# A hybrid decoder layer on one core: which engine evicts the transposes of the second norm, a PSUM bank per tile at the start, and a new order of all instructions

## The chip, the core and the metric

The kernel runs on one core of a Trainium2 chip. The metric is the time of one execution on the device in microseconds (us). The core's engines run side by side and meet at semaphores: TensorE (PE; PEld is its weight load), VectorE (DVE), ScalarE (ACT), GpSimd (POOL) and SyncE (SP), which issues the DMAs. The kernel before has a median of 1169.25 us in 3 runs (1168.5 to 1170.7).

## The reference

One decoder layer on a sequence of 1024 rows of width 1024, in float32. Cut to what matters here:

```python
h = modulate(rms_norm(x), shift1, scale1)            # first norm
q, k, v, z, lx, ly, a, b = split(h @ w_in)           # 4 heads of 128; lx, ly: 512 wide
o = gated_delta_rule_chunked(l2(q), l2(k), v, decay(a), beta(b))   # chunks, state S per head
gdn = rms_norm(o) * silu(z)
xr = conv(lx); r = sigmoid(gate_a(xr)); i = sigmoid(gate_x(xr))
log_a = 8 * r * log_sigmoid(lam)
lru = scan(exp(log_a), sqrt(-expm1(2 * log_a)) * (i * xr)) * gelu(ly)
lru = rms_norm(lru)                                  # over the 512 channels of the group
x = x + gate1 * (concat(lru, gdn) @ w_out)
h2 = modulate(rms_norm(x), shift2, scale2)           # second norm
x = x + gate2 * (relu(h2 @ w_up) ** 2 @ w_down)
out = rms_norm(x)
```

## The kernel before

**Stages.** The kernel works on whole matrices, 128 rows or columns at a time. It normalises x and transposes it on PE (tiles `xTq`, `xTp`) into two rounded halves `hh` and `hl`; projects it, head by head, with three matmuls a product (high by high, low by high, high by low): `k_p`, `z_p`, `q_p`, `v_p`, `lx_p`, `ly_p`; inverts the triangular chunk matrices (`it`, `iy`, `iw`, `iz`: tiny matmuls, with DVE between them); runs the chain of states of each head (`ch`, `cho`, the state `S`, the values `nv`); and for each of four channel tiles the recurrence `lru` (L1377 to L1427): 24 `gate` matmuls, 8 evictions by tanh into `ta` and `ti`, then exp, tanh, square and square root on ACT, products and a scan on DVE, the square of the result (`lsq`) on ACT, and the sum of squares `msum` on POOL. `lrus` (L1452 to L1456) are 8 tiny matmuls over `msum`; they give the factor `rsl` of the norm of the recurrence. The out-projection has a part for the delta rule (`wg`, 16 groups of 12 matmuls) that doesn't need `lrus`, and a part for the recurrence (`wl`, 16 groups of 12), which is multiplied by `rsl` as it is added to x. With two `wl` groups of a row tile t done, `norm2(t)` (L1519 to L1547) squares and scales that tile, transposes it in 8 PE transposes into two PSUM banks of four tiles each (`h2T{t}_0`, `h2T{t}_1`), and evicts each 128x128 tile with scale and shift into `h2r`, the odd ones on ACT and the even ones on DVE. The MLP then runs as seven products of sums of blocks (`upx`, `upy`, `upz`, then `dn`), from 545 us to the end.

**Order.** Nothing is issued as the code stands. Each call appends an `Op` to a `Recorder`, and `schedule` (L293 to L451) lays out all engines with a model: durations, latencies between engines, PE's clock, free buffers. Among the ready operations of an engine it takes the one with the smallest priority, and the priority of each operation that is not part of the backbone on PE is moved by its own entry of `_SHIFTS`, a table of 8374 numbers. `emit` (L453 to L461) issues the operations in the order found, so in the trace nearly every instruction has line L461, groups recorded with `mms` L639; tiles tell them apart. On the chip each engine runs its own queue in that order and stops at the first instruction whose inputs or whose PSUM bank are not free. PSUM has 8 buffers of one bank (`ps`). The names in the rows below end in a running number where a tile is one of several.

**The first transposes.** `xquarter(q, k0)` (L908 to L918) transposes two 128-column tiles of two row tiles of x, four PE transposes into one bank, and evicts each half of the bank twice, once on ACT (`hh`) and once on DVE (`hl`).

Of the kernel before, what the change touches and what calls it, by code (L numbers as in the profile page):

```python
# [13 lines left out]
F32 = mybir.dt.float32  # L14
# [40 lines left out]
OVER = {"DVE": 0.08, "ACT": 0.10, "POOL": 0.03}  # L55
RESERVE = {"b": 11, "ps": 2, "u": 1, "c": 2}
# [67 lines left out]
def dram_box(ap):  # L124
# [7 lines left out]
    'c-p;Nd7MsV|Gw^X&hyL|W8XszB~kViWvT328?qFo^(EON@<v4VvQ(5T*%gHdMTjhg$X@n@A-fqf^UQN!zw4R*&+~qcKYq8*d}cZ4d+z)GF4y<E?&tWOD'  # L132
    ';c&|xskh0cQ>Q>wX@V5F@sDNp1^4&;Sf4GubYUw$h%}(J4>?YOmyZu<3jlpPMN1e=iCq7h&Ra@=488h-GbhBTy?V2@4h)Z`)|A2hFB}BPUhEX;jEdFA0'
    'u6(N3+v1a%Jwxsu3L={WaPMX-G1j+rTZ)9axSIZYow>>z1+6J`ib}&giSGV^?zft<H$B0}}At%?;d~-5Q_rT|9|>1pZ2|#-7+>VKZ$DY)ktRFts8NM8{'
    ';O+JRBBdq&NSDP|NZp%mJnD*9n2s$_TPt&AENY-UCd!8OCuR%d=<y4mR%%vO=Iyu}IFp79<>@tnPmGq=8tZsm<=G8{7ozocEqi?{=;cos*sf^<%1vy2L'
    'CVm7fFy0|~3_r`|o+-3vYM3-YKnqxcPkNjzxWADwq@@E}0+0<u+Xi?4aSw=B5<<FROv!w0H_SyHbZpK@9K3Yk>XvOr%5#+|J_y)h=B_7A~*ocAH%+8V0'
    'n8oGjnN})V2@UPU%n!{)7Bc(cv1Ug7jFP5{bC%a^Uh}LsA~F)UP%fHgYnli%Z5Jd(yJxMA9Lp-feCDO-W6@~lsOS-HW<^s2jWl0rJj7%a(!E!B3Dc3rY'
    'PLHonJRdlSE57lElQdnkii>ll6k|t87-4NG;)rcu-P5pEHIl{8`U|LEo>jBzjN3f>GU)MQPSyU#yFoi$4y(@M26Sexzp`qu41{<8!gS<c9h-1)zJ;vCG'
    'oM%jotjfzRyW!1lqF#AHif>n=i8*dZ3-#*ZUOR>>^xaJ<P?srZz5chXs0NuZXr_0~=PfZrZWY*;vbUT%XaETkPN5s3&h?1zd=1VIA(X9yVoFLvem&r)O'
    '42JAQ75MK9Z4Xd3N=%N)-H`y4xFpHO7ia*3T|3dzs)Sc^rtJyKrYDTswAghO^Q7x3@MLH02ZpbVRtd}eC&yU02FG4tD<oM8KKr@d_RVv_C56WMQZCg0F'  # L140
    'ngN<(jTXYF(fM$U$Hb(LPJT~DX*Ykhf^`$MLsN}|MzF>Fb3pz}2=sX^(if7$%ENT8k6}-Ssct;tO%2UqU(UP_#mu45wt`iAm4T<!Qdf9U#qoQ4G3Nv^-'
    'd$b*s^&2bMFEc0DTHKQL9?E5Z9UT^7cKb+k9<&Yc5%x!m^9;wZG@j;GW$q$7SuyKC%OQL_YiHJZ+rsY1{DLXUo4=I}X_=qcAGFrOc))f*PvjM1l{H_Ym'
    '6wdR*l7&%p(J{`H{5+fiy^!d%lHqs@OLhV9<lpux|fCxZrhNHiwGqQ!HMuo<`ll8W6m<DS0BPyMi@rAYPK0l;9>JU@@VHhIGh7m+^H`#D95jv4}S?S9`'
    ')9n(;S7OwmgzUeQ>8&NC>yZcE<p-2*;R>874nkgc3uJml`_FL8b+kdW}PK(E<f91q}m7y&m?n0B&+3lMulmA@VvQ%vH8yA^b=Rr9Q`Sd8?Xf$@Qp=FVs'
    'Wo2=PWR#myB?H*~t7xIA6Jj9|N4(}V@JQO|uFseBfzh5Q9gaeVEL;2lDfs1PFP*n%;<AdmFJY93}Sl-KMJaXS{9Zrbg`cm=g}S0XGE<)cQXhPTRD$ZT%'
    'okkBq<C7e&_7VBk-TOamg2R0UFj7_MD1L4A<AsC0!UWIT~)WBXY=Pnj8%k4vUlo0u}jo9<H0cYEue8x86i*~2oZl`isbO&Fy{dq=zPtC53#eCZ~*9vxV'
    'j;YJxrU<7P53SIKYb}}IjO8x-w;g6zvkqS6^LB~7AM<&V2h}T!upLVCSzfeO$ambnYdv!;>e`p=Vz}DDD}0N4`Gz7}A8QfP7u|??*jXVqaT(Rziq0}-a'
    'UEXA4)c$xo-oo4qY7_oCmqn8h3uN>8;qJte4DR0tJp|!PI6D$vZjH$ORW2JQhlA`Pth_q4=yp}=EGn+ONhG5Tg%>dHXkzwIDw83`;>4vKRV(w9!5XzW2'
    ')2Iovw<hsJu%=rn=W%;t%!lo%vSSuu*yPwlX`c{$JSXp&T8CX-;|Py7Rhs+I!7&%^`Ea>@xFBQFW0gO<r%O`5C1`Rl*HIS5+&Qm=ewkwJ|$Gzj+(nRtb'
    '~zgq=<|)nH3!0hS^QZ=hW0Rj(dSxyyOfIp7ZB6V7vZOmVmiLs{My35@A^ksjFQW?(c(#xwHPa0W-`q?|ktHl_xiXA6%C1^?z_f#+Junt^Se4Q%ld2Z`-'  # L150
# [1759 lines left out]
```

## Time and profile before

| | |
|---|---|
| median of 3 runs | 1169.25 us |
| the profiled execution's own time | 1167.61 us |
| its span | 1165.8 us |
| mean granted PE clock | 0.99 |
| ACT table loads | 8 |
| matmuls of the MLP | 545 us to 1159 us |

The span is the time from the first to the last instruction of the profile; the rest of the execution, 1.8 us, lies around it. A row of a timeline has start and length in us, engine, line, operation, output and inputs, shapes and count; in brackets stands the idle time of the engine ahead of it and what ended that. A row that stands for several instructions has their total. Matmuls overlap, so the pitch between two starts, not the length, is what a matmul costs.

### The profile page before, as it was taken

The page shows a single profiled execution, that of the slowest core. Times are in us where ns is not written, and L with a number is a line of the kernel's source. Part 1 is how long each engine was busy: PE and PEld are TensorE (multiplying, and loading weights), DVE is VectorE, ACT ScalarE, POOL GpSimd, SP SyncE. Part 2 cuts the span into 40 slices and gives each one's busy share as a digit, 9 for nine tenths or more (in the row PEclk, how much of TensorE's full clock was granted, in tenths as well). Part 3 has the DMA queues.
Part 4 walks back from the last instruction along what each step waited for, and adds up shares of the span by engine and source line. Part 5 has one row for each costly group of instructions (what it writes and reads, how often), then busy time and mean ns, then how long its engine had stood idle before and what let it go on. Part 6 is the DMA issues. An engine that isn't in the chain of part 4 may idle for free.

```text
span 1165.8 us, 16532 instructions
## 1 busy us (share of the span) xinstructions
PE 1139.4 (98%) x6288; PEld 974.9 (84%) x6288; DVE 839.0 (72%) x1143; ACT 613.5 (53%) x961; POOL 275.1 (24%) x161
## 2 busy tenths in 40 slices
PE   8999998999999998999999999999999999999997
PEld 5889997999999987777888888888788888888886
DVE  4749897778878888668776787666794376974663
ACT  5627624354667795367646455445754333352542
POOL 1100101110112325000011142223322057931330
PEclk9999998999999998999999999999999999999999
DMA  9506824355462254032268787768999766865532
GB/s 344 201 12 203 328 86 151 91 166 174 159 199 91 109 219 160 37 134 84 77 208 283 243 304 239 243 208 271 374 405 388 270 233 236 287 228 176 179 137 82
DMA packets 126256, 233.75 MB, mean 200 GB/s; under 512 B 10785, under 2 KB 49886, under 8 KB 126178
## 3 DMA queue, kind: packets, MB, share of 16 engines
q1 hardware_dynamic: 126178, 232.71, 57.5%
q8 instruction: 49, 0.80, 0.3%
q14 instruction: 29, 0.24, 0.1%
HBM read 173.93 MB, written 58.74 MB: 200 GB/s over the span
## 4 chain that ended last, share of the span: by engine, by line
PE 78%; DVE 11%; ACT 6%; issue 2%; POOL 1%; DMA 1%; SPq 0%; POOLq 0%; ACTq 0%; DVEq 0%
PE dn L461 26%; PE upx L461 14%; PE upz L461 7%; PE k_p L461 4%; PE upy L461 4%; PE q_p L461 3%; PE v_p L461 3%; PE wl L461 3%; PE lx_p L461 2%; PE ch L461 2%; PE ly_p L461 2%; PE cho L461 1%; PE wg L461 1%; ACT ta L461 1%; DVE xr L461 1%
## 5 line engine op out<-in xcount | busy, mean ns | idle before, releaser
L461 PE MATMUL upx<-h2h,U 128*128 128x512 f32 x512 | 167.8, 394 | 0.0
L461 PEld LDWEIGHTS upx<-h2h,U 128*128 128x128 f32 x512 | 96.3, 188 | 22.4
L461 POOL TENSOR_TENSOR wd<-wd,wd 128x512 f32<-128x512 f32 x32 | 51.7, 1618 | 255.0 <-DMA wd<-in_w_down_dram 217.9
L461 PE MATMUL upx<-h2l,U 128*128 128x512 f32 x256 | 100.8, 394 | 0.0
L461 DVE TENSOR_TENSOR U<-wu,U 128x512 fp32r<-128x512 f32 x112 | 84.5, 771 | 22.1 <-ACT U L461 21.5
L461 ACT ACTIVATE act<-act 128x512 f32<-128x512 f32 x112 | 69.8, 631 | 44.7 <-DVE act L461 40.8
L461 PE MATMUL upz<-h2h,U 128*128 128x512 f32 x256 | 85.0, 394 | 0.0
L461 ACT CAST U<-wu 128x512 fp32r<-128x512 f32 x112 | 66.5, 616 | 24.7 <-DVE wu L461 16.8
L461 PEld LDWEIGHTS upx<-h2l,U 128*128 128x128 f32 x256 | 48.1, 188 | 11.4 <-issue 0.2
L461 PEld LDWEIGHTS upz<-h2h,U 128*128 128x128 f32 x256 | 48.1, 188 | 11.1
L461 PE MATMUL upz<-h2l,U 128*128 128x512 f32 x128 | 50.4, 393 | 0.0
L461 DVE TENSOR_TENSOR act<-upz,ek 128x512 f32<-128x512 f32 x32 | 22.0, 687 | 37.6 <-PE upz L461 34.2
L461 PE MATMUL upy<-h2h,U 128*128 128x512 f32 x128 | 43.0, 397 | 0.6 <-DVE U L461 0.6
L461 ACT COPY ek<-upx 128x512 f32<-128x512 f32 x48 | 27.7, 583 | 29.0 <-PE upx L461 29.0
L461 DVE TENSOR_TENSOR wu<-wu,wu 128x512 f32<-128x512 f32 x48 | 36.9, 774 | 1.4 <-DMA wu<-in_w_up_dram 1.2
L461 ACT ACTIVATE vn<-ch,bcoef 128x128 f32<-128x128 f32 x32 | 11.6, 365 | 42.0 <-PE ch L461 41.8
L461 PE MATMUL q_p<-hl,q_wh 128*128 128x342 f32 x96 | 33.2, 345 | 0.0
L461 POOL TENSOR_TENSOR fin<-xb,fnw 128x512 f32<-128x512 f32 x11 | 22.2, 2023 | 45.1 <-DVE xb L461 26.9
L461 PE MATMUL q_p<-hh,q_wl 128*128 128x342 f32 x96 | 32.6, 339 | 0.0
L461 PE MATMUL q_p<-hh,q_wh 128*128 128x342 f32 x96 | 32.5, 339 | 0.0
L461 PE MATMUL v_p<-hh,v_wh 128*128 128x342 f32 x96 | 31.9, 333 | 0.0
L461 POOL TENSOR_TENSOR R<-R,R_5o 128x1024 f32<-128x1024 f32 x8 | 23.1, 2887 | 37.1 <-DMA R_5o<-in_w_down_dram 37.1
(587 smaller groups left out, 3622.3 us busy)
## 6 DMA issues: line engine op xcount, KB each, us to landing
L<-aod SPq DMA_DIRECT2D x56, 512.0 KB, 4.3
R<-in_w_down_dram SPq DMA_DIRECT2D x40, 512.0 KB, 7.0
wu<-in_w_up_dram SPq DMA_DIRECT2D x32, 512.0 KB, 5.2
aod<-as SPq DMA_DIRECT2D x64, 256.0 KB, 3.2
wd<-in_w_down_dram SPq DMA_DIRECT2D x32, 512.0 KB, 6.1
aod<-act SPq DMA_DIRECT2D x48, 256.0 KB, 2.1
x<-in_x_dram SPq DMA_DIRECT2D x16, 512.0 KB, 6.0
sc_w<-in_w_mod_dram SPq DMA_DIRECT2D x16, 512.0 KB, 4.3
```

The source lines that it names most:

```text
L461: op.fn(*[res(v) for v in op.a], **{n: res(v) for n, v in op.k.items()})
```

## The change

Four edits.

1. In `norm2` all four tiles of a bank are evicted by one engine: ACT where t + g is odd, DVE where it is even. The number of evictions on each engine stays 32.
2. In `xquarter` each of the two 128-column tiles has a bank of its own, of which half is used.
3. The model in `schedule` charges 1.28 us for a change of function table on ACT (`Op.func`), lets DVE and ACT start later, and puts off an operation on a PSUM bank until the last accesses of the other engines to that bank have ended.
4. `_SHIFTS` is another table, so the order of all engines is another.

```diff
+TABLE = 1.28
...
 _SHIFTS = (
-    'c-p;Nd7MsV|Gw^X&hyL|W8XszB~kViWvT328?qFo^(EON@<v4VvQ(5T*%gHdMTjhg$X@n@A-fqf^UQN!zw4R*&+~qcKYq8*d}cZ4d+z)GF4y<E?&tWOD'
+    'c-p;NXLuFWy8hOhGzcXW30?5es~}a1VCWn`L7Ef+QBXiQqI8rhND~wk2pttfX;OtylwL!ZlF%U}p``8X?Cd@Bo_FWo`{zE-?0Y9a&g99HWY2uF*80l(z'
...
+        op.func = (2 if AF.Sqrt in a else 1 if AF.Exp in a or AF.Tanh in a else 0) if eng == "ACT" else 0
...
+        now["ACT"], now["DVE"] = T_INIT + TABLE, T_INIT + 1.1
+        table, actend = 1, 0.0
+        banks = {}
...
+            bank = [b for b in op.bufs if b.tag == "ps"]
+            at = max((f + lat(ops[j], op) for b in bank for g, (f, j) in banks.get(b, {}).items() if g != e), default=0.0)
+            if at > t + 1e-6:
+                heapq.heappush(fut[e], (at, i))
+                continue
...
+                if op.func and op.func != table:
+                    t, table = max(t, actend + TABLE), op.func
...
+                actend = fin if e == "ACT" else actend
+                for b in bank:
+                    banks.setdefault(b, {})[e] = (fin, i)
...
     def xquarter(q, k0):
-        px = ps(f"xTq{k0}_{q}")
         for i in range(2):
+            px = ps(f"xTq{k0}_{q}{i}")
             for j in range(2):
-                tr(px[:, (2 * i + j) * P:(2 * i + j + 1) * P], xt[2 * q + j][:, (k0 + i) * P:(k0 + i + 1) * P], ident)
+                tr(px[:, j * P:(j + 1) * P], xt[2 * q + j][:, (k0 + i) * P:(k0 + i + 1) * P], ident)
...
-            A.activation(a[:, s], px[:, d], AF.Identity, scale=sc)
+            A.activation(a[:, s], px[:, 0:256], AF.Identity, scale=sc)
...
-                    if j:
+                    if (t + g) % 2:
                         A.activation(rv[:, j, :], pk, AF.Identity, scale=sc, bias=sh)
                     else:
                         V.tensor_scalar(rv[:, j, :], pk, sc, sh, op0=ALU.mult, op1=ALU.add)
```

The instructions are the same in kind and almost in number (5754 matmul rows and 8 table loads on both sides); their order differs on every engine up to the second norm. From the first matmul of the up-projection on, PE's order is the same but for one row. Three places follow, the second of them on two engines.

**Second norm, PE, row tile 1.** Before, PE's queue had the eight transposes of the tile together, among the matmuls `wl21` and `wl30`:

```order
L461 MATMUL wl21_4996<-wo3l_4859,lch01_4694 128x512
L461 MATMUL h2T1_0_5014<-ident_72,h2_1_4985 128x128 x3
L461 MATMUL h2T1_1_5019<-ident_72,h2_1_4985 128x128 x3
L461 MATMUL h2T1_0_5014<-ident_72,h2_1_4985 128x128
L461 MATMUL h2T1_1_5019<-ident_72,h2_1_4985 128x128
L461 MATMUL wl21_4996<-wo3h_4842,lcl01_4845 128x512
```

After, at the same place in PE's queue:

```order
L475 MATMUL wl21_4990<-wo2l_4652,lch01_4691 128x512
L475 MATMUL h2T1_0_5003<-ident_72,h2_1_4966 128x128
L475 MATMUL h2T1_1_5005<-ident_72,h2_1_4966 128x128
L475 MATMUL h2T1_0_5003<-ident_72,h2_1_4966 128x128
L475 MATMUL h2T1_1_5005<-ident_72,h2_1_4966 128x128 x3
L475 MATMUL wl21_4990<-wo2h_4642,lcl01_4697 128x512
L475 MATMUL wl21_4990<-wo3h_4777,lch01_4691 128x512
L475 MATMUL wl21_4990<-wo3l_4848,lch01_4691 128x512
L475 MATMUL wl21_4990<-wo3h_4777,lcl01_4697 128x512
L475 MATMUL h2T1_0_5003<-ident_72,h2_1_4966 128x128 x2
L475 MATMUL wl30_5023<-wo0h_4802,lch00_4552 128x512
```

The last two transposes into bank 0 have moved behind four matmuls of 512 columns; the others stay together.

**Last recurrence, ACT, evictions of the last gates.** Before, ACT's queue from the first of the eight evictions of the last channel tile (`ti3`, `ta3` from `gate300` to `gate35121`) on:

```order
L461 ACTIVATE ti3_4539<-gate301_4513,hxb_693 64x512
L461 ACTIVATE ti3_4539<-gate35121_4528,hxb_693 64x512
L461 ACTIVATE ti3_4539<-gate300_4511,hxb_693 64x512
L461 ACTIVATE ta3_4556<-gate301_4513,hab_691 64x512
L461 ACTIVATE ti3_4539<-gate35120_4526,hxb_693 64x512
L461 ACT_TABLE_LOAD
L461 ACTIVATE ta2_4390<-ta2_4390,c2_769 128x1024
L461 ACT_TABLE_LOAD
L461 ACTIVATE tg3_4506<-tg3_4506 128x1024
L461 ACTIVATE ta3_4556<-gate35121_4528,hab_691 64x512
```

After, ACT's queue ahead of and at the first of them:

```order
L475 CAST xrh3_4545<-xr3_4489 128x1024
L475 CAST lch00_4552<-lcm1_4482 128x512
L475 CAST lch10_4556<-lcm1_4482 128x512
L475 ACT_TABLE_LOAD
L475 ACTIVATE tg3_4511<-tg3_4511 128x1024
L475 ACTIVATE ti3_4583<-gate300_4574,hxb_682 64x512
L475 ACTIVATE ti3_4583<-gate301_4576,hxb_682 64x512
L475 ACTIVATE ta3_4602<-gate300_4574,hab_675 64x512
L475 ACTIVATE ta3_4602<-gate301_4576,hab_675 64x512
L475 ACTIVATE lsq2_4616<-ly2_st_4192 128x1024
```

Both table loads, the square root of the third recurrence (`ta2`) and the tanh of `tg3` now stand ahead of all eight evictions; the square `lsq2` of the third recurrence has come between them.

**Last recurrence, PE, `lrus`.** Before, `lrus` stood ahead of the last 48 of the 192 `wg` matmuls:

```order
L461 MATMUL wg51_4752<-wo7h_4353,gch11_4471 128x512
L461 MATMUL wg51_4752<-wo7l_4372,gch11_4471 128x512
L461 MATMUL wg51_4752<-wo7h_4353,gcl11_4519 128x512
L461 MATMUL lrus_4770<-ones_110,msum_3905 128x1 x8
L461 MATMUL wg60_4786<-wo4h_4133,gch10_4187 128x512
L461 MATMUL wg60_4786<-wo4l_4235,gch10_4187 128x512
```

After, in PE's queue:

```order
L475 MATMUL wg61_4788<-wo4l_4330,gch10_4506 128x512
L475 MATMUL wg61_4788<-wo4h_4239,gcl10_4517 128x512
L475 MATMUL wg61_4788<-wo5h_4393,gch10_4506 128x512
L475 MATMUL lrus_4793<-ones_114,msum_3906 128x1 x8
L475 MATMUL wg61_4788<-wo5l_4404,gch10_4506 128x512
L475 MATMUL wg61_4788<-wo5h_4393,gcl10_4517 128x512
```

It has moved 16 `wg` matmuls down. The last gate matmul has moved too: between it and `lrus` there stand 102 `wg` matmuls now, 136 before.

**First chain, PE.** The first matmul of the chains (`ch0_0`, from the values `nv0` of head 0) stood among the tiny matmuls of the inverse (`iw1`, `iw2`) before:

```order
L639 MATMUL iw1_2173<-aw0_1924,LT_1279 64x64 x3
L639 MATMUL iw2_2146<-aw1_1915,LT_1279 64x64
L461 MATMUL ch0_0_2267<-nv0_2254,LT_1279 128x128
L639 MATMUL iw2_2146<-aw1_1915,LT_1279 64x64 x3
L461 MATMUL q1_p2_2010<-hh6_428,q1_wl_1737 128x342
```

After, in PE's queue:

```order
L475 MATMUL v1_p2_2354<-hh5_497,v1_wh_1742 128x342
L475 MATMUL v1_p2_2354<-hl5_505,v1_wh_1742 128x342
L475 MATMUL ch0_0_2383<-nv0_2351,LT_1324 128x128
L475 MATMUL v1_p2_2354<-hh5_497,v1_wl_2255 128x342
L475 MATMUL v1_p2_2354<-hh6_531,v1_wh_1742 128x342
```

It has moved behind the inverse's last matmuls and a good part of the projection `v1_p2`.

More of the change, by code (lines that the diff above doesn't have):

```diff
@@ L136 @@
[L136 to L150, printed above, removed]
@@ L196 @@
[L196 to L198 removed]
+    'c-p;NXLuFWy8hOhGzcXW30?5es~}a1VCWn`L7Ef+QBXiQqI8rhND~wk2pttfX;OtylwL!ZlF%U}p``8X?Cd@Bo_FWo`{zE-?0Y9a&g99HWY2uF*80l(z'
+    '3-YyCKjQ)H9^YC<D}|VGGY*hW-70qr9Q?AX(@e>h5af*8-~|Y5>aZ0yoxJ0i^cduPN6rpSjBNAd5(1Om6!GE4E{o$gxKWg(p;|MU+VDvb&nP&hCi8+I4'
@@ new lines @@
+    'dC`VMEfv<dnpSq$<ycJe&0Fz_ZiO!jmgKpOD(*MWQDnWld_(^PL!tbZa-#5*OgrjMlPIl&na7fFjZi^HPgIq_~=c9x7P&$j%otpYN9TvI&y$)$>v>3d#'
+    'JGo*8A8q;1Xm*8Lgh-YP8}ZJ&l3h0Q*4@Yy)5loQ_bXfJ1y`r;EzHFl`8>U_$NdTja}1j!z(OFxRu8I!DrX@BzXhVrT9OMOL-b3`kBq0!y<Fyk+ELYiZ'
+    '4dMXxLv&Bk}aCMTl8RKzW*6WTijYxc_%gaFhvV`c-@~%E_EXG5te8~5rCBMYT6x7r{Y>}gBgRLw?>p4;+E7&zjX2=JU*E3(@T=%jfbb_qYC4!IZSlvdh'
+    '>*=oh+N<sw_q12W>G-TmYKqZJCAoh!$E)S~JAFPYQbypR>XLa(^_K~{WM*}>N%qTM))tIa^JQ&zL1VV(Mp`Picvj0i>1oB|v@ubwbAPLPsiaKHx`SO<f'
+    '~l$r(yWTI$2=k(u@&#*4Yfg@$p{&Oe|kn(ORN;sw6^=2WDSr3^0sQC;*EUfY}}IZ@~u9rPDy9!oHbR>Tj#8GnJ&b5cDdiMhGUF(G}@!OF9^H6OY~(aVH'
@@ new lines @@
+    'TB|yzc^u&AQ-u-71HNo<5nCWEryYz{*HXw>D#MW(mo{H@M`Q>;8w^>wZ78k^7*T<=Sk$>rJsztj=-=argi~BHoo`)pk{P|B!jl)j8u$w0FOf9iQFSo#N'
+    '{0nw3$*HxP|7j$3D}1J*-tQ1<Z5f$sCJWA5J=|J(9X=16Y?v%jxy<_bJE_gS?vg0RXe>e}I1ZbryVRPwC#b;9?IO+NK&)}+iw@M0Kdm{&2&{23LkerA~'
+    '3z_o2c9+XG_tc%{7mO_53s%xh8n)^NTmgjF@InP9IPtPUa6f@c<4v#P3)Z(J!F=8E$(ae<p@G-=k%6R=>R~ZuIb6YXKj#3XROw+rGsNupYl*SHxY!;Js'
+    '%$IVq9{bG8Xz#5k$FqY`-Z~4*J=whC9_vfa{L<aabJcuib;BBtR>x;B-$zIV&tB9=g6CHD)a*}vkyb0SKk`~9d>-F+^Fwp5S;3o$3BIn<TDti9Nk!Q!h'
+    'kQ}8Nv39>_KwTCf&JNyef1FR>F-_Zo0)YweYCrSd#k&QtB$L6dfklf=`)dld?;+D`6^2ntDr=Bx?>VDnQINaKYPMa$!zK?ZFaRjl=*nqcf<VMS`5vcoG'
@@ new lines @@
+    '5LinVd7Xn)S@r%=?Zb{|(|X6!&n;w*jl<CSJg0mXbPFvQ-)FkZKLZal}~@Es=-F%UUceXAolr5h<pj2?qE+!{1oVue);2id2TYC10~DM_3oo6#Kb?z39'
+    '(*j<5z`Ju$Gg<2(Z`dP^z_%VCaPTxv)e*&rq^V>9+)CARaoCAf<G@&XY=>q-)-6LFd-@~L#x*Ht&2f^)b)q<KwJtcohX8j9)C%!tx0f{tKIP?_MH##E!'
+    'RJmNhHvs*cxpBB?BgW6ECMB4H1lknkJ`BI`d*9;8c+=t3Xk|0%;KRHY2^Lm&Lmt^AB7L}@Is~}xpO34Wr%EV1;vw9|dq?_)m8mJ|BfQ9O?{Hb>;7kZ(B'
+    ')RT*hb_sbRk1<6JQ%`j<Jx*;=f66G;S-$dj7I`E)6r`NQt2?M6qok9RmJcPbZlvz0@oEe^<tepC-J+j9(@W)`)|}^JW36m4MoV>Lw!W;B*l$DCdexY0V'
+    '6|GH_Nz9sOA0Yl=HNB?fqt&VDr?Glwv}gaqbnm)i;MeMmr-T)MD>eYL9h|b>)M7?mpLjuXr$4`NKuFMSfi=D926CDP-co{G*C|^Lw4#x#zpBC{EM0?(R'
@@ new lines @@
+    '!tERi4W+sbG8}Kk7>Ck}LFVwNR((TPjSKlZL^IBsOTU5h;DygHz$pi*WfyF00#8ovVC?ZTL~9NfIVXwA|!pZ%Q25LSH#76J(_>B|D4~avjr*`sxie&)6'
+    'bfBP=LH#mG@9p`z3>M2c6>!&hpW+)&HaTzNyF2FVR1qphrAt++8n*X6p0%XV3<pX!Y|EGR)&Qe}-As=EG3n(8m4r!18}SP9kSEblW?&d~SEINJ^?PU`d'
+    'LVzMpg_@^9Oggdr4fv24JY_cY&$7ANF)1#_m3kwa&FE*lsW6L1r+<)a9TXc|Ygc1MhIksHMY;k(zacr>^Q`l47%)T;2t_TU@x7*M5C7rQP=g&o~Y(<p4'
+    'B2!gIc9xMcpP!VGNGamjfqPkfA3L7oImZ@_WCyO{37LIw)Req(3nj$^iyb0S!iZI^abJ8qUqK3!U*5wja*-bBgM#uAqS@18_}44+e^d^FJ3Er_7VVrKB'
+    '^+CHlWW*1UD#9h61!_-ri?^!nZ-{^N&y+piVc(P`YzTHmx3i95q7<*s(gr+cd0oRT3(!l+bS#f(NsQ_R#+nk(Nrx*sPs`w*}LM%k<K#%Dv~X|qG}swuv'
@@ new lines @@
+    'PM-H7hO=<<u=>z4eY<)T{L_j8nDsr|Os$rK-tyYLFU6wiC)O@&tl6;lV}bmm+%3RcR`kv+AqQsdK6hXA#UkQQ7gzhcUj+Yxh;h7T~O>;UiT@%1d?i4l^'
+    'bXz50#3Pgb-_g|jP$>9V?uYN2;Zf378u^x%riNH%?NLA6vPrL;QC?w`r;&Ft8#c+WBX{)4kmQXyjKJW^LLkT<m(?bQ(~>U1QtpRSPY2+kEFUMA%nJI1*'
+    'umrz@0kwr%^GYV0Ueap_@N$Mho>{i$zLwJo3mE<|nWSq*6W@ID5Y7eflzfT|wNr8`9V4{&8sw%3dIHjtqY~o2D=_^xtkJb1IC1kGj#Zrk-KkHGf$inOm'
+    'n=x7L%6(?|Na@Z|%CP6BNs4&nE<I;RGj)LaycXxR6w`4)1~Ti561kq@ytGtr6Y=|~0?gk~*0v@J7>-vyiLA#t#wO;Xw`ZU?=eL+XbP=b5Ip1{F-7;4CI'
+    'Chk8RjB+*h7zgTk>wpGY9FG_ZWL47<&IQVjhLmG95n$MaGnndIO^Eyg=32l#-=jY^&>fYOGYJJQmB}_a@CXNEOwHw50`%O2{~sv&lyrd|3+^VW$mw)DX'
@@ new lines @@
+    'Jf1-$;#67s>ej861wz)EVOyh~`UKwKvp9M6jx|gZgehb7v2`Kz=!bU!<1|<{h+pVbx_G?34z~qZ;IMSr|+FO5u1DaS2rzwPyGVpU{tI@eseMin3V^l*e'
+    'i^F|?w3owMvOUXFdAI?bfgQ1XDYtjnKG__H{_Z_3Nk$S7tE)w9$I6i`ad<4i+y>ciQQSKN%K)8kFY7PZI_*D)St$aD;8C5_oD!nu|@suSyOI;N^c>PuB'
+    'vpH`PuW!Bj~=}M~s*lF}qpX(d!JojZhJ8cFt)}Md%ICCH5KXf=B>3gDf5c9n?^S2-IzJhEaKPezzs2)^K_1Q(Msn@6zqNpJHs-u`qbQ+>cQ)Ry{v8p(c'
+    '=Sy0zlXzSsw+WF;a)zq3lXPd_jgVDpu(}}Gw8+BOQiSNSTy9Z)G$Hm?X6~%yXUSF#=Kc$2;83!Z^Qfn4Qq6wM%(;%L^x_d_{6c{IcAU(@EUJ(1nB!q;7'
+    'Iohs6)YbhckH1$Yp?QuASVByhf9caCEzAob87Q27n$~qHvjtX-v<#$f{5^%nN)+!uL2Ru&xb4Xr<Mab80BM3n(*3zGKjW$h)5>#IvzEc)#V(SlO0<`vK'
@@ L199 @@
+    'O#iqFC42<SEs2;XnVI)|;dRy>OE}Jq>=v){^Wo4zu{zd@AS>oS$Fs)Mn0wN!y&A^s)Gw+`{SMLItk31eMrY$MbB32h>gpn1S~k+xnl&`QOk#0O#*NnRt'
+    'tOuQB~#I<^gGO&IbNs}SngSK~3B3_Y4UE86k68_7SWGiDWKlH+kpaiw#~T4FKCd=*8>x;tUM)t-E02DMy_tY_RCF%O<FhRvisabz#^CYdNY53`Ab9?T('
+    'k>ny+G7svB%%FgcBd*R}BZ2KzJ!T)56Q(F&qs~ya)L29UDe|;!%(goEdPDQHk<!#kTddo1?P1Tp;x+RrktO{pk)g(ek${an|F+gOZuiByNtJOKX5YFp6'
+    'TQyguBp$KWJaH2togST}rVP<1Q4?d-K($Gf+Tr*fh16+PQ#<E96D5<l+=%G*5VzD!T~_@YT0j&&'
 )
@@ L225 @@
     __slots__ = ("adj", "work", "port", "eng", "fn", "a", "k", "outs", "ins", "dur", "bb", "preds", "succs", "allocs", "bufs", "lst", "ready",
-                 "need", "load", "bias", "pri", "tiny", "tail")
+                 "need", "load", "bias", "pri", "tiny", "tail", "func")
 class Recorder:
@@ L908, in xquarter @@
     def xquarter(q, k0):
-        px = ps(f"xTq{k0}_{q}")
         for i in range(2):
+            px = ps(f"xTq{k0}_{q}{i}")
             for j in range(2):
-                tr(px[:, (2 * i + j) * P:(2 * i + j + 1) * P], xt[2 * q + j][:, (k0 + i) * P:(k0 + i + 1) * P], ident)
-        for i in range(2):
+                tr(px[:, j * P:(j + 1) * P], xt[2 * q + j][:, (k0 + i) * P:(k0 + i + 1) * P], ident)
             a, b = hT[k0 + i]
-            s, d, sc = slice(q * 256, q * 256 + 256), slice(i * 256, i * 256 + 256), A1[:, k0 + i:k0 + i + 1]
-            A.activation(a[:, s], px[:, d], AF.Identity, scale=sc)
-            V.scalar_tensor_tensor(out=b[:, s], in0=px[:, d], scalar=sc, in1=a[:, s].bitcast(F32),
+            s, sc = slice(q * 256, q * 256 + 256), A1[:, k0 + i:k0 + i + 1]
+            A.activation(a[:, s], px[:, 0:256], AF.Identity, scale=sc)
+            V.scalar_tensor_tensor(out=b[:, s], in0=px[:, 0:256], scalar=sc, in1=a[:, s].bitcast(F32),
                                    op0=ALU.mult, op1=ALU.subtract)
```

81 lines of the change are left out of this document (30 added, 51 removed).

## The prediction

> **What bounds the kernel now.** The first view is the page's table of busy time, since it says whether any engine is full; the second is the list of what PE waited for, since that engine is the full one.
>
> ```profile
> PE 1139.4 (98%) x6288; PEld 974.9 (84%) x6288; DVE 839.0 (72%) x1143; ACT 613.5 (53%) x961; POOL 275.1 (24%) x161
> ```
>
> ```profile
> PE lrus L461 <- POOL msum L461: 3.8, 1, 3.8
> PE ch L461 <- DVE nv L461: 3.0, 1, 3.0
> PE h2T L461 <- ACT h2r L461: 2.9, 7, 0.7
> PE warm L461 <- DVE ones L461: 2.3, 1, 2.3
> PE h2T L461 <- DVE h2r L461: 1.7, 3, 0.7
> PE cho L461 <- issue: 1.3, 1, 1.3
> PE it L639 <- DVE xnc L461: 0.9, 1, 0.9
> PE sc_r L461 <- DMA sc_w<-in_w_mod_dram: 0.8, 1, 0.8
> ```
>
> The columns of the second are total, times and longest, in us. PE is the bound, and the change neither adds nor removes a matmul, so all that it can win is time in which PE stands still or runs slowly, and all that it can lose is new time of that kind. The eight rows add up to 16.7 us: 3.8 at `lrus`, 4.6 at `h2T`, 3.9 around the inverse and the first chain, 4.4 elsewhere. Busy time hides a second loss, which the windows show. Their columns are the stretch, its length, busy time of PE, PEld, DVE, ACT and POOL, then the granted clock of PE, the DMA share and GB/s.
>
> ```profile
> 179.45:182.86 3.41, 3.41 (x13) 2.63 (x13) 3.28 (x5) 2.95 (x5) 0.00 (x0) 0.50 0.80 267
> 196.52:206.76 10.24, 10.24 (x55) 9.39 (x55) 3.29 (x6) 2.14 (x4) 0.00 (x0) 0.50 0.17 54
> ...
> 459.34:466.17 6.83, 6.83 (x21) 5.58 (x21) 1.99 (x3) 4.37 (x7) 6.83 (x4) 0.50 0.74 269
> ...
> 545.00:850.00 305.00, 304.19 (x1312) 245.86 (x1311) 221.60 (x297) 175.84 (x295) 66.67 (x40) 1.00 0.71 242
> ```
>
> In the first three stretches PE is fully busy at half clock, so half of each is lost: 1.7, 5.1 and 3.4 us. The second begins after the wait for `nv`, the third right after the wait for `msum`; a wait there is paid twice. The last row is the first half of the MLP: 304.19 of 305 us busy at full clock. There is nothing to win there, PE's order in it stays, and the term for it is zero. The whole prize is in the first 545 us, and at most some 27 us.
>
> **The change part by part.** *Evictions of the second norm.* The rows of one row tile, PE and ACT:
>
> ```profile
> 485.53 0.39 PE L461 MATMUL wl<-wo0h,lch 128*128 128x512 f32 x1
> ...
> 485.76 0.39 PE L461 MATMUL wl<-wo0l,lch 128*128 128x512 f32 x1
> ...
> 486.23 0.82 PE L461 MATMUL h2T<-ident,h 128*128 128x128 f32 x6
> 486.65 0.89 ACT L461 ACTIVATE h2r<-h2T,sh,sc 128x128 f32<-128x128 f32 x2
> ...
> 487.61 0.44 PE L461 MATMUL h2T<-ident,h 128*128 128x128 f32 x2 [0.56 <-DVE h2r L461]
> ```
>
> Six transposes go out; then evictions begin on the banks, and the two transposes left stand until ACT and DVE have let go of their bank. Ten such waits make the 4.6 us. With one engine to a bank an eviction no longer waits for the other engine's, and in the new order the transposes that are late stand behind four `wl` matmuls, at a pitch of 0.23 us (485.53 to 485.76) some 0.9 us of work, against two ACT evictions of 0.89 us in the row of 486.65. The cover is thus just long enough; where it isn't, the wait is a few tenths, and it may still come ten times. A bank is now drained in series: four ACT evictions by that row are 1.8 us where two engines took half of it. The cost is hidden by the `wl` groups, each of 12 matmuls or 2.8 us; the eight PSUM buffers decide if it isn't. Bounds: no gain, since such waits could only be renamed, and −6.2 us, the ten waits and 0.16 us of restart at each. I take **−4**.
>
> *The wait for `lrus`.* The last gate matmuls on PE, then ACT, DVE and POOL:
>
> ```profile
> 421.97 0.40 PE L639 MATMUL gate<-xrh,gw 64*128 64x512 f32 x2
> ```
>
> ```profile
> 427.54 1.28 ACT L461 ACT_TABLE_LOAD   x1
> 428.83 1.06 ACT L461 ACTIVATE ta<-ta 128x1024 f32<-128x1024 f32 x1
> ...
> 432.29 1.96 ACT L461 ACTIVATE ta<-gate,hab 64x512 f32<-64x512 f32 x3
> 434.29 1.25 ACT L461 ACTIVATE aa<-ta,nc 128x1024 f32<-128x1024 f32 x1
> 435.57 1.25 ACT L461 ACTIVATE ta<-ta,c 128x1024 f32<-128x1024 f32 x1
> 436.72 1.04 ACT L461 ACTIVATE a<-aa 128x1024 f32<-128x1024 f32 x1
> ...
> 442.40 1.05 ACT L461 CAST wo2h<-wo 128x1024 fp32r<-128x1024 f32 x1 [3.69 <-DVE wo L461]
> ...
> 446.25 2.17 ACT L461 CAST lch<-lcm 128x512 fp32r<-128x512 f32 x4
> ...
> 454.52 1.06 ACT L461 ACTIVATE lsq<-ly_st 128x1024 f32<-128x1024 f32 x1 [2.93 <-DVE ly_st L461]
> ```
>
> ```profile
> 437.79 1.23 DVE L461 SCALAR_TENSOR_TENSOR ta<-a,ta 128x1024 f32<-128x1024 f32 x1 [1.59 <-ACT a L461]
> 438.93 3.44 DVE L461 SCALAR_TENSOR_TENSOR wo<-wo,cols,g_bc 128x1024 f32<-128x1024 f32 x1
> 442.29 0.68 DVE L461 TENSOR_TENSOR x<-wg,x 128x512 f32<-128x512 f32 x1
> 442.89 0.68 DVE L461 TENSOR_SCALAR ta<-ta 128x1024 f32<-128x1024 f32 x1
> ...
> 447.60 1.72 DVE L461 TENSOR_TENSOR xr<-xr,ta 128x1024 f32<-128x1024 f32 x1
> ...
> 450.43 2.28 DVE L461 TENSOR_TENSOR_SCAN xr<-aa,xr 128x1024 f32<-128x1024 f32 x1
> ...
> 453.21 1.21 DVE L461 TENSOR_TENSOR ly_st<-ly_st,xr 128x1024 f32<-128x1024 f32 x1
> ```
>
> ```profile
> 455.72 2.35 POOL L461 TENSOR_TENSOR msum<-msum,lsq 128x1024 f32<-128x1024 f32 x1 [7.49 <-ACT lsq L461]
> ```
>
> ```profile
> 458.12 2.49 PE L461 MATMUL lrus<-ones,msum 128*128 128x1 f32 x16 [3.77 <-POOL msum L461]
> ```
>
> From the end of the last gates (422.3) to `lrus` (458.1) the chain takes 35.8 us, and 136 `wg` matmuls at 0.23 us cover only 32 of them. In the new order 102 stand there, 23.7 us, so the chain must lose 12 us to keep PE busy. Added up along the new order: four evictions at 0.65, 2.6; `wo2h` 1.05; `aa`, `a`, tanh 3.5; the product `ta` 1.23; an addition to x and the maximum 1.4; the root 1.06, its table load lying beside DVE's work behind two `lch` casts (1.1 + 1.28 against 1.23 + 1.4); four additions to x begun under the root, 2.7 less 1.06, 1.7; the product with xr 1.72; a cast's remainder 0.68; scan 2.28; an addition 0.68; `ly_st` 1.21; `lsq` 1.06; `msum` 2.35. That is **22.5**. What is gone is what stood in the chain before: two loads with a root and a tanh between the gate evictions (4.7 us), and three scalings `wo` between `ta` and the scan, one of them 3.44 us, which now stand ahead of or behind it. The margin is 1.2 us; hand-offs between engines, seven of them, eat most of it. If it holds, the 3.77 us go and the 3.4 us of half clock with them. DVE's additions to x wait for `wg` groups, but such a group is done before PE gets to `lrus`. I take **−6.5**; bounds −7.2 and, by the old length of the chain, 35.8 − 23.7 = 12.1 us of waiting, which is +8.3.
>
> On the table loads the Trainium skill (ScalarE: Activation LUTs, What ACT_TABLE_LOAD costs) says that a switch takes 1283 ns for the load and about 1380 ns of draining. The trace agrees on the load and not on the rest: the load at 427.54 ends at 428.82, and the root starts at 428.83. By the skill's figure the chain in the new order would grow by about 1.2 us and the margin would be gone, a wait of about 1 us; I go by the row.
>
> *The inverse and the first chain.*
>
> ```profile
> 195.02 0.46 PE L461 MATMUL ch<-nv,LT 128*128 128x128 f32 x2 [2.99 <-DVE nv L461]
> ```
>
> PE's queue reached `ch0_0` before DVE had made `nv0`; behind it waited tiny matmuls of the inverse, and then followed 10.24 us at half clock. Now `ch0_0` stands among projections, some 12.8 us further down if the matmuls ahead of it are counted at the pitches of the trace, while DVE has only a few more short instructions ahead of `nv0` (copies `LT`, the split `q2_wl`). So this wait should go. But the inverse's tiny matmuls (`iw`, `iz`) now lie more to themselves ahead of it, or between more projections, and one or two windows at half clock may come there. Waits 3.9, half clock 6.8: bounds 0 and −10.7; as it is half of it that I can trace, **−5**.
>
> The Trainium skill (TensorE: Matmul & The Clock Gate, Part 1) has the clock decided in free-running windows of 3413 ns. The three stretches, 3.41, 10.24 and 6.83, are one, three and two such windows, so the trace agrees. By it a wait of unchanged length can cost a window more or less as the phase falls, 1.7 us each way on this term.
>
> *First transposes.* A bank per tile: the same four transposes and four evictions, and the two tiles no longer bar each other. Its wait doesn't stand among the eight; DMAs and DVE decide the start. The `sc_r` wait of 0.8 and the projections' first start are the bounds, 0 and −3; SP's loads are in another order, I take **−1**. `warm` is unchanged.
>
> *Model.* `TABLE`, `Op.func` and `banks` run on the host and cost the chip nothing. *New order elsewhere.* 8374 new numbers move everything ahead of the MLP. The chain waits of now (`cho`, 1.3) may go, others come; the eight rows hold 4.4 us that no term above takes, and a little over half of that is my allowance for new ones: **+2.5**, bounds −2 and +6.
>
> Sum: −4 − 6.5 − 5 − 1 + 2.5 = −14. Against the profiled execution's own 1167.6 that gives 1153.6; the median stands 1.6 above that execution, so **1155**.
>
> **The rivals.**
>
> *Half of it.* The second norm gains its 4, the start 1, new waits cost 2.5; `lrus` still waits 3.6 us because the hand-offs add up, but keeps full clock, so 3.6 is won; the inverse wins nothing. −6.1: **1163**. For it speaks the margin of 1.2 us.
>
> *All waits go.* −4.6 − 7.2 − 10.7 − 0.8 = −23.3: **1146**. Against it speaks that every new order has waits of its own.
>
> *Slower, by `lrus`.* If the chain keeps its 35.8 us, PE comes to `lrus` early and stands 12.1 us: +8.3, with −4 − 1 + 2.5 and nothing from the inverse, +5.8: **1175**. It decides from a wait of 3.8 + 2.5 = 6.3 us on, a chain of 30. For it speaks that each engine's queue holds other work whose inputs, as `lch` from a DMA or `lsq2`, may be late; against it the rows above.
>
> *The order is not what the chip sees.* If DVE and ACT lag behind the model as they do now, the waits only change names: **1169**.
>
> **How the numbers follow.** Forecast 0.50, its own range 1148 to 1162; half 0.20; all 0.10; slower 0.14; unchanged 0.06. A measurement of this kernel can tell about 0.2%, 2.3 us, from no change. Faster: the first three less a little, 0.79; same 0.06; slower 0.15. The range, 1143 to 1170, takes in the forecast, half, all and unchanged, and leaves out most of the slower case.
>
> **What would show it.** Right: `h2T` rows under 1 us in PE's waits; no wait at `lrus` over 1 us and full clock behind it; no wait of `ch` for `nv`, and at most two windows at half clock between 150 and 210 us; the MLP as long as before. Wrong: a wait at `lrus` above 6 us, or a new row above 3 us in PE's waits ahead of 545 us.

## The result and the profile after

The changed kernel takes **1151.74 us** (median of 4 runs, 1149.7 to 1152.9), the kernel before 1169.59 us in the 4 runs beside it: a ratio of 0.9845, 95% interval 0.9828 to 0.9862, 17.9 us less. The profiled execution of the changed kernel is its fastest run, 1149.7 us with a span of 1147.8; against that of before (1167.6) it is 17.9 us less too.

The page's busy row and the list of what PE waited for, of the changed kernel:

```profile
PE 1135.8 (99%) x6288; PEld 971.7 (85%) x6288; DVE 823.0 (72%) x1143; ACT 611.0 (53%) x961; POOL 274.8 (24%) x161
```

```profile
PE warm L475 <- DVE ones L475: 2.3, 1, 2.3
PE sh_c L475 <- DVE sh_acc L475: 0.9, 1, 0.9
PE crow_ps L475 <- DMA crow<-in_c_dram: 0.9, 1, 0.9
PE kk L475 <- DVE k3T L475: 0.5, 1, 0.5
```

The rows for `lrus` (3.8), `ch` (3.0), `h2T` (4.6), `cho` (1.3) and `it` (0.9) are gone; `sh_c` and `crow_ps` are new. The windows at half clock (columns as before: stretch, length, busy times, clock, DMA share, GB/s) are two ahead of the last matmul, 6.8 us in all, where there were 20.5:

```profile
36.79:40.20 3.41, 3.41 (x18) 3.41 (x18) 1.48 (x4) 0.96 (x2) 1.46 (x1) 0.50 1.03 400
197.21:200.63 3.42, 3.42 (x14) 3.42 (x14) 3.07 (x4) 1.01 (x2) 0.00 (x0) 0.50 0.88 290
455.80:460.00 4.20, 4.16 (x26) 3.77 (x27) 3.85 (x6) 3.04 (x5) 1.93 (x1) 1.00 0.72 242
```

The last row is the place behind `lrus`: full clock. The second norm now, PE, ACT and DVE:

```profile
481.78 0.82 PE L475 MATMUL h2T<-ident,h 128*128 128x128 f32 x6
482.31 0.81 ACT L475 ACTIVATE h2r<-h2T,sh,sc 128x128 f32<-128x128 f32 x2 [1.09 <-PE h2T L475]
482.35 0.48 PE L475 MATMUL wl<-wo2h,lcl 128*128 128x512 f32 x1
482.64 1.05 DVE L475 TENSOR_SCALAR h2r<-h2T,sc,sh 128x128 f32<-128x128 f32 x3 [1.68 <-PE h2T L475]
...
483.13 0.39 PE L475 MATMUL wl<-wo3h,lcl 128*128 128x512 f32 x1
483.36 0.38 PE L475 MATMUL h2T<-ident,h 128*128 128x128 f32 x2
```

Six transposes, four `wl` matmuls, and the last two transposes at 483.36 without a wait: ACT had let go of their bank at 483.12. Not every row tile looks like this. By PE's rows, five of the eight have their last one or two transposes behind two to five `wl` matmuls; the other three have all eight together, as the fourth:

```profile
495.11 1.04 PE L475 MATMUL h2T<-ident,h 128*128 128x128 f32 x8
...
495.86 1.51 ACT L475 ACTIVATE h2r<-h2T,sh,sc 128x128 f32<-128x128 f32 x4 [0.80 <-PE h2T L475]
```

There the first eviction begins when the last transpose does, and PE doesn't wait either. And the chain to `lrus`, PE and POOL:

```profile
431.54 0.40 PE L653 MATMUL gate<-xrh,gw 64*128 64x512 f32 x2
...
455.35 0.40 PE L475 MATMUL wg<-wo5h,gch 128*128 128x512 f32 x1
455.85 1.95 PE L475 MATMUL lrus<-ones,msum 128*128 128x1 f32 x16
```

```profile
452.37 3.42 POOL L475 TENSOR_TENSOR msum<-msum,lsq 128x1024 f32<-128x1024 f32 x1 [9.83 <-ACT lsq L475]
```

From the last gates (431.94) to the end of `msum` (455.79) it took 23.9 us, 35.8 before, and PE came to `lrus` at about the same moment. The margin was zero, not 1.2 us.

### The profile page after: what moved, and what is told of

It is laid out like the page before. It is cut to its first block, busy times and chain, and to the rows that moved or that the text cites. A ratio compares the mean times of both kernels' runs of the same rounds, so it can differ in the third digit from the quotient of the medians.

```text
span 1147.8 us, 16549 instructions
## 1 busy us (share of the span) xinstructions
PE 1135.8 (99%) x6288; PEld 971.7 (85%) x6288; DVE 823.0 (72%) x1143; ACT 611.0 (53%) x961; POOL 274.8 (24%) x161
## 4 chain that ended last, share of the span: by engine, by line
PE 83%; DVE 7%; ACT 6%; issue 2%; DMA 1%; POOL 0%; SPq 0%; POOLq 0%; DVEq 0%; ACTq 0%
PE dn L475 27%; PE upx L475 16%; PE upz L475 8%; PE k_p L475 4%; PE wl L475 4%; PE upy L475 4%; PE v_p L475 3%; PE q_p L475 3%; PE lx_p L475 2%; DVE xr L475 2%; PE ch L475 1%; PE cho L475 1%; ACT ta L475 1%; DVE xx L475 1%; DVE ftmp L475 1%
## 5 line engine op out<-in xcount | busy, mean ns | idle before, releaser
L475 ACT CAST U<-wu 128x512 fp32r<-128x512 f32 x112 | 66.5, 616 | 25.0 <-DVE wu L475 14.3
L475 PEld LDWEIGHTS upz<-h2h,U 128*128 128x128 f32 x256 | 48.1, 188 | 11.6 <-issue 0.2
L475 POOL TENSOR_TENSOR xb<-xb,keep 128x512 f32<-128x512 f32 x8 | 13.9, 1745 | 81.9 <-DVE keep L475 81.9
L475 PE MATMUL v_p<-hl,v_wh 128*128 128x342 f32 x96 | 31.7, 330 | 0.0
L475 PE MATMUL lx_p<-hl,lx_wh 128*128 128x342 f32 x96 | 31.6, 329 | 0.0
L475 PE MATMUL ly_p<-hh,ly_wh 128*128 128x342 f32 x96 | 31.5, 328 | 0.0
```

Source lines behind the costliest of these rows:

```text
L475: op.fn(*[res(v) for v in op.a], **{n: res(v) for n, v in op.k.items()})
```

## The experiments

In all of them every engine keeps the order of the kernel that is named, so that an edit moves only what its diff says; the diffs are shortened to that. The kernel before was measured again beside each group of experiments, with medians of 1170.8 to 1171.9 us; a ratio, and a gain worked out from it, is to its runs in the same group.

### The eviction edit alone, in the old order

```diff
-                    if j:
+                    if (t + g) % 2:
```

> The kernel before with its order on every engine kept, and only the engine of the 64 evictions of the second norm changed to one per bank. Theory (the eviction edit and the order are both needed): some transposes still stand right behind evictions of their own bank, so of the 4.6 us of h2T waits 1 to 3 us stay, and the time falls by 2 to 5 us, to 1164 to 1167. Rival (the eviction edit alone does it): h2T waits under 1 us and 6 to 7.5 us won, 1162 to 1163. Second rival (the waits only change names): within 1 us of the kernel before.

Measured: 1171.24 us against 1170.8, ratio 1.000 (0.998 to 1.002). PE's waits of that run:

```profile
PE h2T L482 <- ACT h2r L482: 2.6, 6, 0.6
...
PE h2T L482 <- DVE h2r L482: 1.9, 4, 0.8
```

Ten waits and 4.5 us, as before. The rows of one tile show why:

```profile
484.84 0.82 PE L482 MATMUL h2T<-ident,h 128*128 128x128 f32 x6
485.26 0.73 DVE L482 TENSOR_SCALAR h2r<-h2T,sc,sh 128x128 f32<-128x128 f32 x2
...
486.05 0.44 PE L482 MATMUL h2T<-ident,h 128*128 128x128 f32 x2 [0.39 <-DVE h2r L482]
```

One engine drains the bank now, but it drains it while PE still has a tile of that bank to write, and PE waits for it. Of the three expectations only the second rival held: nothing is won that this interval, of 2 us to each side, would show.

### The old evictions, in the new order

```diff
-                    if (t + g) % 2:
+                    if j:
```

> The changed kernel with its order on every engine kept, and only the evictions of the second norm given back to two engines per bank (odd tiles ACT, even tiles DVE). Theory (both needed): h2T waits of 2.5 us or more come back, 1154.5 to 1158. Rival (the new order of the transposes alone does it): h2T waits under 1 us, 1151 to 1153.

Measured: 1152.33 us (ratio 0.9833, 0.9805 to 0.9862); the changed kernel had 1151.74 and 0.9845 in its own group. One `h2T` row of 0.4 us is left:

```profile
PE h2T L496 <- ACT h2r L496: 0.4, 1, 0.4
```

The rival holds: the order does it. By PE's waits the edit of the evictions is worth some tenths of a microsecond; by the times it can't be told from nothing. Which trait of the order does it, the `wl` matmuls between the transposes or evictions that begin later, was not separated.

### Sixteen matmuls ahead of `lrus`, in the old order

```diff
-MATMUL lrus x8
 MATMUL wg60 x12
 MATMUL wg61 x4
+MATMUL lrus x8
```

> The kernel before with 16 of the wg matmuls that stand behind lrus on PE put ahead of it, nothing else moved. Theory (the wait is a matter of place, since the factor that lrus gives is not urgent, and the half clock behind it is its consequence): 16 times 0.23 = 3.7 us of work cover the wait of 3.8, the wait is under 0.5 us, PE keeps full clock, and 6 to 7.5 us are won: 1162 to 1163.5. Rival (the chain to lrus sets the end, not its place): the first wl groups wait for rsl instead, and the time stays within 1.5 us. Second rival (the half clock has another cause): wait gone, 6.83 us of half clock stay, 3.8 us won.

Measured: 1164.53 us, ratio 0.9943 (0.9925 to 0.9962), 6.7 us less. The `lrus` row is gone from PE's waits, and behind it the clock is full, while the 10.24 us near 200 us stay:

```profile
455.00:470.00 15.00, 14.89 (x73) 12.06 (x72) 12.87 (x16) 6.07 (x9) 12.12 (x6) 1.00 0.60 211
198.63:208.87 10.24, 10.24 (x55) 9.41 (x55) 3.29 (x6) 2.12 (x4) 0.00 (x0) 0.50 0.19 64
```

The theory holds. About half of what this place wins is clock: 3.8 us of waiting and 3.4 of half speed. The other profiles bear it out: in all four with this wait (3.3 to 3.8 us) 6.83 us of half clock lie at it, and in the nine without it there are none in seven and 3.41 us in two, the second and the last experiment of this section.

### `nv0` ahead of three DVE instructions, in the old order

```diff
-TENSOR_SCALAR ssqq<-ssqq
-TENSOR_TENSOR q0_dm<-qk0_1,q0_dm
-TENSOR_TENSOR q0_dm<-qk0_0,q0_dm
 TENSOR_TENSOR nv0<-vtok0_0,ncoef
 TENSOR_TENSOR nv0<-vtok0_1,ncoef
+TENSOR_SCALAR ssqq<-ssqq
+TENSOR_TENSOR q0_dm<-qk0_1,q0_dm
+TENSOR_TENSOR q0_dm<-qk0_0,q0_dm
```

> The kernel before with the two halves of nv0 put ahead of one ssqq and two q_dm instructions on DVE, nothing else moved. Theory (the wait of PE for nv0 causes the half clock behind it): the wait falls from 3.0 to 0.8 us or less, at least one of the three windows at half clock goes, and 4 to 7.5 us are won: 1162 to 1165.5. Rival (the tiny matmuls of the inverse bring the half clock, whatever the wait): the wait falls alike, 10.24 us of half clock stay, 2 to 2.5 us are won: 1167.

Measured: 1161.45 us, ratio 0.9932 (0.9904 to 0.9961), 8.0 us less by the ratio. The first matmul of the chains and the stretch around it:

```profile
193.54 0.49 PE L493 MATMUL ch<-nv,LT 128*128 128x128 f32 x2 [0.57 <-ACT aw L493]
```

```profile
176.00:210.00 34.00, 32.41 (x501) 29.93 (x494) 27.98 (x40) 15.63 (x25) 2.63 (x1) 1.00 0.47 154
```

A wait of 3.0 us became one of 0.6, and in this execution all 13.65 us of half clock of that stretch were gone. The theory holds for the 10.24 us right behind the wait: all four profiles with a wait of 2.7 to 3.0 us here have them, and none of the nine without it. The other 3.41 us, which had begun ahead of the wait, can't be its consequence: the profiles of the first and the fifth experiment have the wait and not this stretch, that of the seventh has the stretch (at 181.33 us) and not the wait. Nor is the gain there in every execution: the nine spread from 1158.2 to 1171.1 us, and two of them, at 1170.6 and 1171.1 with a mean granted clock of 0.985 and 0.986 where the other seven had 0.994 to 0.997, won nothing. Where those two lost it no profile shows. The changed kernel takes this wait away by moving `ch0_0` down; that move alone was not tried.

### The new order from the first `wl` on

```diff
+HEAD = the first 3840 of 8374 operations, in the order of the kernel before
...
-        order = self.schedule()
+        order = HEAD + [i for i in self.schedule() if i not in HEAD]
```

> The order of the kernel before up to the first wl matmul, the new order of all engines from there on; both code edits are in. So of the change only the second norm and what follows it are new. Theory (the new order of the transposes, not the engine of an eviction, takes the h2T waits away): h2T waits under 0.5 us, 5.5 to 8 us won against the kernel before, 0.993 to 0.9955 of its time; the lrus and nv waits of 3.8 and 3.0 us stay. Rival (the gain at the second norm needs the earlier order too): under 3 us won.

Measured: 1159.38 us, ratio 0.9901 (0.9878 to 0.9923), 11.6 us less (9.0 to 14.3), more than the theory gave. There is no `h2T` row, and the old waits stay:

```profile
PE lrus L580 <- POOL msum L580: 3.4, 1, 3.4
PE ch L580 <- DVE nv L580: 2.8, 1, 2.8
```

In the profiles the way from the first `wl` to the last matmul of the up-projection took 364.1 us, 364.0 in the changed kernel and 371.7 in the kernel before: 7.6. Here are the first `wl`, the first matmul of the up-projection and its last one, of the kernel before and of the changed one:

```profile
474.38 0.39 PE L461 MATMUL wl<-wo0h,lch 128*128 128x512 f32 x1
529.71 0.39 PE L461 MATMUL upx<-h2h,U 128*128 128x512 f32 x1
846.07 0.39 PE L461 MATMUL upz<-h2h,U 128*128 128x512 f32 x1
```

```profile
465.14 0.40 PE L475 MATMUL wl<-wo0h,lch 128*128 128x512 f32 x1
514.95 0.39 PE L475 MATMUL upx<-h2h,U 128*128 128x512 f32 x1
829.11 0.39 PE L475 MATMUL upz<-h2h,U 128*128 128x512 f32 x1
```

The rest may come from executions that this profile of before doesn't show: the same way took 376.8, 375.4 and 371.7 us in the first, third and fourth experiments, which have the old order there too, and 364.0 to 366.2 in all profiles with the new one. With the old order the profiles of two experiments, the first and the third, have 3.3 and 3.4 us of waiting for `U` at `upy`, where that of before has 0.6; here is the third's:

```profile
PE upy L488 <- DVE U L488: 3.4, 2, 2.8
```

The new order from `wl` on has no such row. How often the old one pays those 2.8 us was not counted.

### The old order for the start

The same kind of list, 700 operations long, to the middle of the k projections, ahead of the new order; measured twice, the second time beside the changed kernel.

> The changed kernel with the order of the kernel before for the first 700 of 8374 operations (to the middle of the k projections, some 65 us), the new order from there on. By the starts of PE's work the changed kernel was 5.3 us behind the old one there. Theory (the new order of the start is worse in itself, with a window at half clock at 37 us): 2.5 to 5.5 us won against the changed kernel, 1146 to 1149. Rival (the old start was ahead only because its clock rose earlier in that one execution): within 1.5 us of the changed kernel, 1150.5 to 1153.

> The changed kernel itself, beside the next two on the same chip: 1150 to 1153 us, no h2T and no lrus row over 0.5 us, windows at half clock near 37 us and perhaps others.

> The kernel with the old start again, beside the changed kernel on the same chip: 3 to 6 us below it (theory: the new start costs that); rival: within 1.5 us of it.

Measured: 1146.55 us the first time (1144.8 to 1148.6; ratio to before 0.979, 0.9767 to 0.9814). The changed kernel itself was not in that group; its twin with one bank at the start (below) was, and is 4.5 us above. The second time 1148.91 us (1145.6 to 1149.9), and the changed kernel beside it 1151.57 (1151.1 to 1152.7): 2.7 us less, just under the 3 that were expected, and no run of the one reaches the other. The theory holds, near its lower end: the new start is 2.7 to 4.5 us worse. The gain doesn't need a clock that rises early: with the old start the low clock of the first microseconds ended at 14.8 and 16.0 us in the two profiled executions, with the new one at 12.9 to 15.0 us in four; even so the last `k_p` matmul began at 95.5 and 96.2 us with the old start and at 98.4 to 99.2 with the new one. The `sc_r` rows of the first profile show the late clock, where two products take 1.01 us that take 0.59 at full clock:

```profile
13.11 1.01 PE L518 MATMUL sc_r<-sc_w,cact 128*1 128x256 f32 x2
14.78 0.59 PE L518 MATMUL sc_r<-sc_w,cact 128*1 128x256 f32 x2
```

The window at half clock near 37 us was in three of the four profiles with the new start and in none of those with the old one. What in the start brings it was not tried.

### The three places together, in the old order

The list of 3840 operations with the two edits by hand, `lrus` and `nv0`, in it.

> The kernel of the new order from wl on, and in the old order ahead of it the two edits by hand of the earlier runs: nv0 ahead of three DVE instructions, 16 wg matmuls ahead of lrus. Theory (the three places hold all that the new table wins, and their gains add): 6.3 + 8 + 7 = 21 us won against the kernel before, 0.980 to 0.984 of its time, the changed kernel's time or 1 to 4 us below it. Rival (the gains overlap, since each shifts the phase of the clock's windows): 13 to 17 us won.

Measured: 1147.66 us, ratio 0.9799 (0.9775 to 0.9823), 23.6 us less, where the three alone give 6.7 + 8.0 + 11.6 = 26.3. They add up but for a part that is inside the intervals. So two moves by hand and the new order from `wl` on give more than the whole new table: it wins about the same behind its start (the old start with the new rest had 1146.55 us in this group, 1.1 less than the three places) and gives 2.7 to 4.5 us back at the start.

### The two tiles of `xquarter` in one bank again, in the new order

```diff
-            px = ps(f"xTq{k0}_{q}{i}")
+            px = first[:, 256 * i:256 * i + 256]
```

> The changed kernel with its order kept and the two tiles of xquarter in one bank again. Theory (a bank per tile is worth nothing by itself): within 1 us of the changed kernel, 1150.7 to 1152.7. Rival (the second tile's transposes wait for the first one's evictions): 1 to 2.5 us slower, with a row of xTq in PE's waits.

Measured: 1151.02 us (ratio 0.9822, 0.9795 to 0.9849), and no `xTq` row; the changed kernel had 1151.74 and 1151.57 in two other groups. The bank per tile is worth nothing that this can measure.

### The `sh2_c` products spread out

```diff
-MATMUL sh2_c x8, in two blocks among the matmuls of the chains
+MATMUL sh2_c, one behind every third projection matmul from the sixteenth on
```

> As the kernel with the old start, but the eight sh2_c products of one column (one wait of 0.9 us and 12 of 16 matmul rows in a block at 327 us in that run, with 6.8 us of half clock behind them) are put one by one between projection matmuls some 3 to 15 us later. Theory (the wait and the block bring the window at half clock): the sh_c row goes from PE's waits, no half clock near 330 us, 1.5 to 4.5 us won against the kernel with the old start of the same call. Rival (such windows come and go with the phase of the clock and the block is only where one fell): 0.5 to 1.5 us won.

Measured: 1147.96 us (1147.1 to 1149.0) beside 1148.91 of the old start in that group, 0.95 us less and within the spread of both. The wait of 0.9 is gone, and near 330 us the clock is full, but new waits came instead and a window at half clock lay elsewhere:

```profile
PE ch L562 <- DVE r L562: 1.2, 1, 1.2
PE upx L562 <- ACT ek L562: 0.9, 1, 0.9
```

```profile
326.00:337.00 11.00, 9.60 (x68) 8.59 (x67) 7.17 (x12) 9.14 (x16) 1.64 (x1) 1.00 0.00 0
454.31:457.72 3.41, 3.41 (x10) 2.63 (x9) 3.03 (x5) 1.57 (x4) 3.41 (x3) 0.50 0.12 41
```

The rival's size is what was measured. The best versions are those with the old start, with or without this edit, the three places in the old order among them.

## Why the prediction was right, and where not

**The bound** was read rightly in the main: the gain is time in which PE stood or ran at half clock, and of the 18.0 us between the two profiles 14.8 lie ahead of the first matmul of the up-projection (529.71 and 514.95 us above). The zero for the MLP was too small. The up-projection took 316.4 us before and 314.2 after, because two of the `h2T` waits, the 0.6 us of `upy` and 0.2 us at `g_r` stood inside it, and PE's order there is not the same but for one row: the transposes of the last row tiles and the `g_r` products have moved. The down-projection, from its first to its last `dn` matmul, was 1.0 us shorter without a wait in either (308.6 against 309.6); the other profiles lie between, so that this is not clear of scatter.

**The second norm: size and cause were off.** I put it at −4 with −6.2 as the far bound (its 0.16 us of restart is a matmul's length of 0.39 less the pitch of 0.23). From the first `wl` to the end of the up-projection it was −7.7 in the two profiles, 5.5 of them ahead of the up-projection, and −11.6 in the time of the fifth experiment. The step that failed is "with one engine to a bank an eviction no longer waits for the other engine's": one engine to a bank was worth nothing, since what PE waited for was not the quarrel of ACT and DVE but any eviction of a bank into which it still had to write. The order from `wl` on carried the gain. Part of it is the other half of that paragraph, the late transposes behind `wl` matmuls, though four of them stand so in one row tile alone, two to five in five of the eight, and none in three. I had the order before me and still gave the edit the first place, since it was the one visible in the code. The Trainium skill (PSUM — Partial Sum Buffer, PSUM bank collisions raise a hardware error) says that engines must be kept apart by bank and not by address, a reader from a reader too. The traces show this kernel keeping to the first: with one engine to a bank the write of another tile still waited 0.39 us. What would happen without it no run here shows. The far bound was short because ten waits and their restarts are not all: the waits at `upy` and `g_r` went as well.

**`lrus`: right in size, by less than I thought.** −6.5 forecast; moving it by itself gave −6.7. The chain was put at 22.5 us and took 23.9; two terms were too small: `msum` with 3.42 us, where the row that I used had 2.35, and the evictions, since `lsq2` (1.06 us, at 431.92) stands between them, as the order showed, and I left it out. The rest came out 0.8 us shorter. With 23.7 us of `wg` that is no margin, so the slower rival was nearer than its 0.14, though a wait of one or two microseconds there would, I estimate, have cost only that and perhaps a window of 1.7 us. The price of the table load stayed open: DVE was later than the load in the new order, so that nothing waited for it.

**The inverse and the first chain: right, half its size.** Forecast −5; `nv0` first, by itself, gave −8.0. The same stretch of the kernel before and of the changed one:

```profile
150.00:215.00 65.00, 60.46 (x722) 56.83 (x721) 51.41 (x85) 22.20 (x36) 2.95 (x1) 0.89 0.36 114
```

```profile
150.00:215.00 65.00, 64.73 (x751) 60.46 (x750) 51.81 (x87) 26.19 (x39) 2.37 (x1) 0.97 0.35 110
```

Busy time by clock is 53.8 us of work at full speed before and 62.8 now, 9 more. I took half of the possible 10.7 for want of evidence on what brings the half clock. The profiles with and without the wait show that it brings the 10.24 us: I could have read it from the order in time of the two, as I did at `lrus`.

**The start: wrong in sign.** "SP's loads are in another order, I take −1": it is +2.7 to +4.5. I looked at the waits only; the new order has the `crow` wait (0.9) and, in three of four profiles, the window at 37 us (1.7). These two make 2.6; what else there is was not found.

**New waits**: +2.5 forecast; `sh_c` and `crow` are 1.8.

So that 1155 came as near as it did to 1151.7 is in part luck: the 9 us forecast for the second norm and the inverse, where 16 to 20 were measured, stood against a loss that I hadn't seen. What was measured at the three places, 26.3 us singly and 23.6 together, less 2.7 to 4.5 at the start, gives 19.1 to 20.9, where the change as a whole won 17.9, and 19.4 in the later group.

## What to carry to other kernels

A PSUM bank that several instructions fill should be filled before its draining begins, or have its late writers stand behind other work: an order that does so took away 4.6 us of waiting, and the choice of the evicting engine took away none. Two waits of 3.0 and 3.8 us on PE, with half clock behind them, were worth 8.0 and 6.7 us here, so look at the granted clock behind each wait, and first move the one instruction that is waited for. When a large table of an order is replaced, test its stretches against the old ones: the old start with the new rest beat both kernels.

## What the runs showed of the hardware that was not expected

The clock of the first 16 us differs between executions of the same order. With the old start two `sc_r` products took 0.59 us from 9.47 us on in the profile of the kernel before; in that of the second run of the old start they took 1.00 to 1.01 us from 9.82 up to 15.14 us. That is some 6 us at half clock, or 3 us of time, more than several of the effects studied here. The stretches at half clock have the lengths 3.41, 6.83 and 10.24 us wherever they fall ahead of the last matmul, in all thirteen profiles. The Trainium skill (TensorE: Matmul & The Clock Gate, Part 1) has free-running windows of 3413 ns, and the lengths in the traces agree. A stretch near 330 us, behind the `sh_c` products, was in four of the six profiles with that order and not in the first one of the changed kernel, so a single profile doesn't tell whether a place is safe from it.
